# Encoder layer on one core: 30 convolution taps of one channel quarter as ScalarE copies with accumulating transfers, the output bank in halves, and other shares of the softmax scalings

## The chip, the cores and the metric

The kernel runs on one core of a Trainium2 chip. The metric is the device time of one execution in microseconds (us). Five engines work side by side: TensorE (PE: products and transposes into PSUM), VectorE (DVE), ScalarE (ACT), GpSimd (POOL) and SyncE (SP). Here POOL and SP mostly issue transfers (DMA). Each engine runs its own instructions in order and waits on semaphores for the others.

## The reference

One layer of a streaming encoder for 16 meta tokens, 1024 prompt frames and a stream of 32 sample frames, 1024 channels, float32. The change touches two of its parts, the depthwise convolution over a GLU and the attention over chunks of 64 frames:

```python
z = h @ w_in                                  # h = rmsnorm(x); all projections in one
glu = a_in[..., :D_CONV] * jax.nn.sigmoid(a_in[..., D_CONV:])          # 512 channels
y = depthwise_causal_conv(glu_ext, dw_w, dw_b)                         # 31 taps for each channel
conv = jax.nn.silu(layernorm(y, ln_g, ln_b))
s = q . k * HEAD_DIM ** -0.5 + bias            # 8 heads, 2 key heads; 16 meta + 3 x 64 keys
m = jnp.maximum(jnp.max(s, axis=-1, keepdims=True), sink)
p = jnp.exp(s - m)
denom = jnp.sum(p, axis=-1, keepdims=True) + jnp.exp(sink - m)
o = (p / denom) @ v
x = x + concat(conv, o) @ w_out               # then a gated feed-forward part and a last norm
```

The sink enters as one more key column. The attention of the meta tokens and that of the sample stream are jobs of their own, with a few keys each.

## The kernel before, in words

Everything lies channel by channel: a channel is a partition, the T = 1072 tokens run along the row, in three blocks of 336, 384 and 352. A float32 product is made of three passes over values split in a high and a low part (L239 hi x hi, L240 lo x hi, L241 hi x lo). A weight is split by `wsplit` (L221 to 230): ScalarE copies raw to whi (L224) and minus that to wlo (L228), and a transfer on POOL's queue adds raw onto wlo in memory (L229, an accumulating transfer).

The stages, by the time of the profile: input, statistics and first projections to 50 us; projections 50 to 168; attention 168 to 252, with the last projections between its steps; output projection and the convolution's norm 252 to 345; start of the feed-forward part 345 to 375; feed-forward 375 to 1030; its last norm and the stores to 1069.

Projections. `in_group` (L581) makes one output tile of 128 channels for one block of tokens, 24 products of some 3.9 us in all, in one of three PSUM banks called mm. VectorE takes the bank out later: L508 and L513 for the GLU, L533 for the queries (qp, with qm and qs for the meta and sample tokens). For the 512 convolution channels, in four quarters p, the GLU result lies in `glu[:, p]` and the sum over taps in `acc[:, p]`. `conv_taps` (L355 on) makes a quarter's taps ready: tap 0 is one operation acc = glu * w0 + b (L362), each further one acc = glu shifted * wk + acc (L365), on VectorE. `taps` (L370) gives them out after each group, at a low priority, so that VectorE's order, which a scheduler makes, fills them in between other work. SEGS says how a quarter is cut along the tokens: quarters 0 to 2 are one piece of 1090 columns (1072 and gaps between the streams), quarter 3 three pieces of 324, 384 and 382. The attention keeps its probabilities in the memory of `glu[:, 0]` and `glu[:, 1]`, so the taps of quarters 0 and 1 must be given out before it (L661).

Attention. The jobs (Meta, 11 chunks, Sample, 5 chunks) go through a pipeline of three steps (loop L937 to 969). In round i, job a of the round before gets its reciprocal (L701) and scalings: of its four tiles of probabilities, SCA[i] are scaled on ScalarE (L706) and the rest on VectorE (L704). The new job gets its scores S (PE, L732; Meta L786), the row maxima m on VectorE (L689, into sm) and the exponentials on ScalarE (L696). Job z of the round before that gets its output products (PE, L767 and L771; Meta L802) into a PSUM bank o. Then a is transposed (PE, L751 and L753 into pt; Meta L793), ScalarE copies the transposes (L758; Meta L796), and copies z's output from o into CA (`keep`, L775). FILL[i] pieces of the projection of the last two weights follow as work for PE, then taps for VectorE. There is one bank o, so a chunk's first output product waits for the copy of the chunk before. CA (128 x 4 x 1072) holds the attention output and is not used before the first `keep`. L546 is a sigmoid of 1040 columns between them, which changes ScalarE's function table there and back.

The orders of PE and ScalarE are written out by hand, as the program runs; those of VectorE, POOL and SP come from a scheduler with priorities. Statistics of a norm (`rms_steps`, L243 on) go over stat (L253 to 257), ScalarE's diag (L260) and a product R (L263).

Of the kernel before, what the change touches and what calls it, by code (L numbers as in the profile page):

```python
# [10 lines left out]
F32 = mybir.dt.float32  # L11
F32R = mybir.dt.float32r
AF = mybir.ActivationFunctionType
ALU = mybir.AluOpType
# [3 lines left out]
P = 128  # L18
# [6 lines left out]
T = NPR + NS  # L25
# [4 lines left out]
CW = 31  # L30
# [36 lines left out]
WLD = True  # L67
MANUAL = {mybir.EngineType.PE, mybir.EngineType.Activation}
MANEND = MANUAL | {mybir.EngineType.DVE}
SCA = [1, 3, 3, 3, 1, 1, 3, 2, 3, 3, 3, 1, 2, 3, 0, 1, 1, 3, 2, 2]  # L70
LN0 = 14
LNS = 21
FILL = [4, 6, 6, 2, 3, 3, 6, 1, 3, 3, 1, 4, 5, 0, 3, 6, 0, 3, 0, 3]
ORDER = [2, 3, 8, 9, 4, 5, 10, 11, 12, 13, 6, 7]
SEGS = (((0, 1, 2),), ((0, 1, 2),), ((0, 1, 2),), ((0,), (1,), (2,)))
CSD = ['12', '00']
AH = (1, 2, 1, 3, 5, 4, 5)
AG = (('00', '02'), ('h',), ('l',), ('10',), ('12',))
# [78 lines left out]
def body(nc, tc, cp, wp, xp, dp, io):  # L157
# [13 lines left out]
    def new(pl, name, *shape, dt=F32):  # L171
        return pl.tile([P, *shape], dt, tag=name, name=name)
# [7 lines left out]
    def pcol(name, i):  # L180
        o, _ = PRM[name]
        return prm[:, o + i:o + i + 1]
# [13 lines left out]
    acc = new(pc, "acc", NCV, ACCW)  # L196
    cG, pg = pool("glu", "left")
    glu = new(pg, "glu", NCV, EXTW)
# [81 lines left out]
    pa = cPS.__enter__()  # L280
# [51 lines left out]
    CA = new(pc_, "ca", 4, T)  # L332
# [24 lines left out]
    def conv_taps(p, a0, a1, b):  # L357
        e, a = glu[:, p, :], acc[:, p, a0:a1]

        def tap(k):  # L360
            if k == 0:
                nc.vector.tensor_scalar(out=a, in0=e[:, a0:a1], scalar1=pcol("cw", p * CW), scalar2=pcol("cb", p),  # L362
                                        op0=ALU.mult, op1=ALU.add)
            else:
                nc.vector.scalar_tensor_tensor(out=a, in0=e[:, a0 + k:a1 + k], scalar=pcol("cw", p * CW + k),  # L365
                                               in1=a, op0=ALU.mult, op1=ALU.add)

        tapq.append([b, a1 - a0, tap, 0, p])

    def taps(us, behind=None):  # L370
        spare[0] += us
        with tc.high_priority(offset=-1000000):
            while tapq and spare[0] > 0:
                spare[1] = (spare[1] + 1) % min(WAYS, len(tapq))
                ch = tapq[spare[1]]
                if behind:
                    with tc.issue_after(behind):
                        ch[2](ch[3])
                else:
                    ch[2](ch[3])  # L380
                ch[3] += 1
                if ch[3] == CW:
                    tapq.remove(ch)
                spare[0] -= (ch[1] + 120) / 960
        if not tapq:
            spare[0] = 0.0
# [96 lines left out]
    def in_mm(b, w, lead=0):  # L483
        n = TB[b][1] - lead
        hv, lv = (z.rearrange("p (a b) -> p a b", a=KD) for z in w)
        ps = mmt()[:, :n]
        for k in range(KD):
            mm3(ps, [k], lambda k: hv[:, k, :], lambda k: lv[:, k, :], lambda k: HI[b][:, k, lead:],
                lambda k: LO[b][:, k, lead:], k == 0, k == KD - 1)
            for g, at in zip(rms1, RM):  # L490
                if slot[0] in at:
                    next(g)
            slot[0] += 1
            yield ps

    def lead(c, b):
        return H0 if c >= 10 and b == 0 else 0
# [46 lines left out]
    def gate_all(p):  # L544
        for a, n in ((CW - 1, NPR), (CW - 1 + SOFF, NS)):
            nc.scalar.activation(glu[:, p, a:a + n], glu[:, p, a:a + n], AF.Sigmoid)  # L546
        for b in range(3):
            for lo_, hi_, o in pieces(b, CW - 1, SOFF):
                g = glu[:, p, o:o + hi_ - lo_]
                defer.append((g, rb[b][:, lo_:hi_]))  # L550

    def taps_of(p, b):
        for seg in SEGS[p]:
            if seg[-1] == b:
                conv_taps(p, OB[seg[0]][0], OB[b][0] + AW[b], seg[0])
        if b == 2:
            nc.sync.dma_start(d.cap[p], glu[:, p, NPR:NPR + CW - 1])
            nc.sync.dma_start(d.cas[p], glu[:, p, EXTW - CW + 1:EXTW])
# [5 lines left out]
    def undefer():  # L564
        while defer:
            g, rs = defer.pop(0)
            nc.vector.tensor_tensor(out=g, in0=g, in1=rs, op=ALU.mult)

    def flush():
        undefer()  # L570
        while pend and pend[0][1] in ready:
            c, b, ps = pend.pop(0)
            if c % 2:
                undefer()
            in_evac(c, b, ps)
            if c < 8 and c % 2:
                taps_of(c // 2, b)
            if c in (4, 6) and c in ORDER[NPRE:] and b == 2:
                gate_all(c // 2)

    def in_group(c, b, w, us=0.0):  # L581
        for ps in in_mm(b, w, lead(c, b)):
            pass
        flush()
        taps(us, gate[-1].ins if gate else None)
        pend.append((c, b, ps))

    def win(c):
# [69 lines left out]
    for _ in vr:  # L658
        pass
    flush()  # L660
    while any(t[4] < 2 for t in tapq):  # L661
        taps(1.0, gate[-1].ins)
    nc.sync.dma_start(d.kmp, kT[:, 0:NMETA])
# [45 lines left out]
        return pa.tile([P, 2, 256], F32, tag="s2", name="S", bufs=2)  # L709

    def o_tile():
        return pa.tile([P, 512], F32, tag="o", name="o", bufs=1)

    pts = [pa.tile([P, 2, 256], F32, tag=f"pt{i}", name=f"pt{i}") for i in range(2)]
    for q in pts:
        nc.vector.memset(q, 0.0)

    class Chunk:
# [43 lines left out]
        def outs(self):  # L762
            self.o = o_tile()
            c, m, n = self.c, self.m, self.n
            for kv in range(2):
                ks = slice(kv * 64, kv * 64 + 64)
                nc.tensor.matmul(self.o[ks, :256], va[:m, c, ks], ptb[kv][:m, 0, :], start=True, stop=n == m)  # L767
            for kv in range(2):
                ks = slice(kv * 64, kv * 64 + 64)
                if n > m:  # L770
                    nc.tensor.matmul(self.o[ks, :256], vb[:n - m, c - 1, ks], ptb[kv][:n - m, 1, :], start=False,  # L771
                                     stop=True)
# [5 lines left out]
    class Meta(Chunk):  # L778
# [19 lines left out]
        def outs(self):  # L798
            self.o = o_tile()
            for kv in range(2):  # L800
                ks = slice(kv * 64, kv * 64 + 64)
                nc.tensor.matmul(self.o[ks, :64], va[:16, 0, ks], ptb[0][:16, 0, kv * 64:kv * 64 + 64], start=True,  # L802
                                 stop=True)
# [4 lines left out]
    class Sample(Meta):  # L808
# [19 lines left out]
        def outs(self):  # L828
            self.o = o_tile()
            for kv in range(2):  # L830
                ks = slice(kv * 64, kv * 64 + 64)
                nc.tensor.matmul(self.o[ks, :128], vsa[:, ks], ptb[1][:, 0, kv * 128:kv * 128 + 128], start=True,
                                 stop=False)
            for kv in range(2):
                ks = slice(kv * 64, kv * 64 + 64)
                nc.tensor.matmul(self.o[ks, :128], vsb[:48, ks], ptb[1][:48, 1, kv * 128:kv * 128 + 128],
                                 start=False, stop=True)
# [73 lines left out]
    def ah_add(m2, i, b, ps):  # L911
        m, (t0, n) = 2 * m2 + i, OB[b]
        nc.scalar.copy(X[b][:, m, :], ps)
        if i == 1:
            nc.gpsimd.dma_start(X[b][:, m - 1:m + 1, :], d.xT[:, m - 1:m + 1, t0:t0 + n], accum_op=ALU.add)
# [17 lines left out]
    a, z = None, None  # L933
# [3 lines left out]
    for i in range(len(jobs) + 2):  # L937
        job = jobs[i] if i < len(jobs) else None
        if a:
            a.soft_b(SCA[i])  # L940
        if job:
            job.scores()
            job.soft_a()
            job.exps(0)
            job.exps(1)
        if z:
            z.outs()
        if a:
            a.trans()
            a.probs()  # L950
        if z:
            z.keep()
            kept[0] = i - 2
        for _ in range(min(FILL[i], left)):
            next(stream)
            left -= 1
        flush()
        taps(TA[i], (job or a or z).q[1][3])
        if not left and not pend and not defer:
            for _ in stream:  # L960
                pass
            next(later, None)
            ticks = len(jobs) + 2 - i
            for _ in range(AH[-ticks] if ticks <= len(AH) else 0):
                next(ahs, None)
            for q in adds:
                ah_add(*q)
            adds.clear()
        z, a = a, job
    for _ in later:  # L970
        pass
# [157 lines left out]
    with tc.tile_pool(name="psB", bufs=1, space=PSUM, reuse_waits="tile") as pf:  # L1129
# [332 lines left out]
        def scr(n):  # L1462
            nscr[0] += 1
            return scrs[nscr[0] % len(scrs)][:, :n]
# [62 lines left out]
        for i, (m, b) in enumerate([(m, b) for m in range(KD - 1, -1, -1) for b in (1, 2)] +  # L1527
# [6 lines left out]
            t0, n = YB[b]  # L1534
# [72 lines left out]
        for pos, (t0, n) in enumerate(ENDS):  # L1607
            last = pos + 1 == len(ENDS)
            for m in range(KD):
# [6 lines left out]
                to = parts[0] if m == 0 else scr(n)  # L1616
# [108 lines left out]
```

## Time and profile before

| | |
|---|---|
| three runs | 1068.04, 1068.41, 1074.01 us; median 1068.41 |
| the profiled execution | 1070.42 us, its span from first to last instruction 1068.6 |
| mean granted TensorE clock | 0.995 |
| bytes moved by DMA | 116.81 MB, 109 GB/s in the mean |
| chain of work that ended last | PE 58%, DVE 5%, DMA 2%, ACT 2% |

A row of the window view is one stretch of the time: its length, the busy time of each engine with its instructions in brackets, TensorE's granted clock as a share of full speed, the busy share of the 16 DMA engines, and GB/s. A row of the groups view names line, engine, operation, output and inputs with their shape, then the number, the busy time with the mean of one in ns, and the idle time ahead of it. A row of the waits view reads: engine, what it was about to do, what it waited for, total us, times, longest. A row of the timeline gives start and length, and in brackets the idle time ahead and who ended it. A row of the transfers view: target and source, queue, number, KB each, and the us from issue to landing.

### The profile page before, as it was taken

What the parts mean: (1) busy time and instruction counts of PE and PEld (TensorE: products, weight loads), DVE (VectorE), ACT (ScalarE), POOL (GpSimd) and SP (SyncE); (2) the same over time, 40 slices, a digit from 0 to 9 for tenths busy, and PEclk for the clock granted to TensorE, in tenths of its full rate; (3) what the DMA queues carried; (4) which work ended last, traced back from release to release, by engine and by line L of the source; (5) the groups of instructions that cost most, each with busy time, mean ns of one, the idle gap of its engine ahead of it and who ended that gap; (6) DMA issues with size and microseconds to landing.
All of it is one profiled execution on the core that took longest, in us unless ns stands there. A gap on an engine that the chain in (4) does not pass through costs nothing.

```text
span 1068.6 us, 19869 instructions
## 1 busy us (share of the span) xinstructions
PE 1041.1 (97%) x7737; PEld 1011.6 (95%) x7737; DVE 872.6 (82%) x1622; ACT 488.2 (46%) x1043; POOL 159.3 (15%) x189
## 2 busy tenths in 40 slices
PE   8999999989999999999999999999999999999996
PEld 7999997768999999999999999999999999999996
DVE  7799999999978988888888887888778865986635
ACT  8532225997676644433333343343337622532332
POOL 1112000001425112001000100100101041000042
PEclk9999999999999999999999999999999999999998
DMA  8343332114863122243233234233226894732104
GB/s 269 82 105 90 90 88 61 40 34 76 161 169 107 48 91 90 70 138 94 70 120 112 65 101 131 67 101 110 92 81 204 259 188 99 245 120 80 60 18 146
DMA packets 67030, 116.81 MB, mean 109 GB/s; under 512 B 10224, under 2 KB 43240, under 8 KB 66936
## 3 DMA queue, kind: packets, MB, share of 16 engines
q1 hardware_dynamic: 57112, 97.44, 29.2%
q0 software_dynamic: 9536, 17.89, 10.0%
q8 instruction: 61, 1.00, 0.4%
q14 instruction: 33, 0.27, 0.1%
q10 hardware_dynamic: 288, 0.22, 0.1%
HBM read 78.90 MB, written 27.51 MB: 100 GB/s over the span
## 4 chain that ended last, share of the span: by engine, by line
PE 58%; DVE 5%; DMA 2%; ACT 2%; issue 1%; POOL 0%; POOLq 0%; DVEq 0%; SPq 0%; ACTq 0%
PE mm L1208 49%; PE mm L239 3%; PE mm L240 3%; PE mm L241 3%; DMA rbg<-yq 1%; DVE traw L1225 1%; DVE x L1345 1%; DMA raw<-wdn 0%; DVE x L1595 0%; DVE bl L1145 0%; DMA x<-yq 0%; DVE tl L1145 0%; PE R L263 0%; DVE sl L1145 0%; ACT bh L1144 0%
## 5 line engine op out<-in xcount | busy, mean ns | idle before, releaser
L1208 PE MATMUL mm<-bh,sl 128*128 128x264 f32 (+1 forms) x912 | 215.0, 285 | 0.4 <-DVE x L1345 0.4
L365 DVE SCALAR_TENSOR_TENSOR acc<-glu,prm,acc 128x1090 f32<-128x1090 f32 (+3 forms) x180 | 168.0, 968 | 0.4
L1208 PEld LDWEIGHTS mm<-bh,sl 128*128 128x128 f32 x912 | 157.6, 189 | 0.7 <-DVE x L1345 0.7
L1208 PE MATMUL mm<-th,rawr 128*128 128x266 f32 (+1 forms) x640 | 121.3, 285 | 0.0
L1208 PE MATMUL mm<-bl,sl 128*128 128x264 f32 (+1 forms) x424 | 120.9, 285 | 0.0
L1208 PE MATMUL mm<-bh,wlo 128*128 128x264 f32 (+1 forms) x440 | 118.0, 285 | 0.0
L1345 DVE TENSOR_TENSOR x<-x,mm 128x264 f32<-128x264 f32 (+7 forms) x238 | 76.4, 347 | 50.3 <-PE mm L1208 50.2
L1208 PE MATMUL mm<-bh,whi 128*128 128x264 f32 (+1 forms) x440 | 113.1, 285 | 1.3 <-DVE x L1345 1.3
L239 PE MATMUL mm<-hi,whi 128*128 128x352 f32 (+3 forms) x312 | 104.6, 335 | 0.2 <-ACT hi L274 0.2
L240 PE MATMUL mm<-lo,whi 128*128 128x352 f32 (+3 forms) x312 | 102.1, 327 | 1.7 <-DVE lo L275 1.7
L241 PE MATMUL mm<-hi,wlo 128*128 128x352 f32 (+3 forms) x312 | 101.6, 326 | 0.0
L1208 PEld LDWEIGHTS mm<-th,rawr 128*128 128x128 f32 x640 | 101.2, 189 | 0.0
L1208 PE MATMUL mm<-th,sl 128*128 128x264 f32 (+1 forms) x352 | 93.1, 285 | 0.5 <-DVE x L1345 0.5
L1208 PE MATMUL mm<-tl,rawr 128*128 128x266 f32 (+1 forms) x320 | 91.4, 286 | 0.0
L1208 PEld LDWEIGHTS mm<-bh,wlo 128*128 128x128 f32 x440 | 80.7, 189 | 0.0
L1208 PEld LDWEIGHTS mm<-bh,whi 128*128 128x128 f32 x440 | 79.0, 189 | 1.7 <-DVE x L1345 1.3
L1208 PEld LDWEIGHTS mm<-bl,sl 128*128 128x128 f32 x424 | 79.9, 189 | 0.0
L1208 PE MATMUL mm<-bl,whi 128*128 128x264 f32 (+1 forms) x272 | 77.4, 285 | 0.0
L1208 PEld LDWEIGHTS mm<-th,sl 128*128 128x128 f32 x352 | 64.2, 189 | 0.6 <-issue 0.6
L1144 ACT CAST sl<-x 128x512 fp32r<-128x512 f32 (+1 forms) x41 | 29.7, 726 | 76.1 <-DMA x<-wup 40.3
L240 PEld LDWEIGHTS mm<-lo,whi 128*128 128x128 f32 x312 | 59.1, 189 | 3.4 <-DVE lo L275 3.1
L239 PEld LDWEIGHTS mm<-hi,whi 128*128 128x128 f32 x312 | 59.0, 189 | 1.7 <-ACT hi L274 0.7
(346 smaller groups left out, 2898.9 us busy)
## 6 DMA issues: line engine op xcount, KB each, us to landing
x<-wup SPq DMA_DIRECT2D x20, 512.0 KB, 4.4
x<-wup SPq DMA_DIRECT2D x40, 256.0 KB, 2.8
yq<-x SPq DMA_DIRECT2D x32, 264.0 KB, 2.8
wlo<-raw POOLq DMA_DIRECT2D x16, 512.0 KB, 4.5
raw<-win SPq DMA_DIRECT2D x12, 512.0 KB, 3.6
raw<-wdn SPq DMA_DIRECT2D x12, 512.0 KB, 3.8
rb<-yq SPq DMA_DIRECT2D x10, 528.0 KB, 4.4
yq<-gx SPq DMA_DIRECT2D x16, 264.0 KB, 4.7
```

Of the source, the lines that this page charges most:

```text
L239: nc.tensor.matmul(ps, whi(k), xhi(k), start=first and i == 0, stop=False)
L240: nc.tensor.matmul(ps, whi(k), xlo(k), start=False, stop=False)
L241: nc.tensor.matmul(ps, wlo(k), xhi(k), start=False, stop=last and i == n - 1)
L365: nc.vector.scalar_tensor_tensor(out=a, in0=e[:, a0 + k:a1 + k], scalar=pcol("cw", p * CW + k), in1=a, op0=ALU.mult, op1=ALU.add)
L1144: nc.scalar.copy(hi, raw)
L1208: nc.tensor.matmul(ps, w[:, j, :], x[:, j, :], start=first and j + i == 0, stop=j == 3 and i == 2, skip_group_check=True)
L1225: nc.vector.scalar_tensor_tensor(out=out[:, lo_:hi_], in0=x, scalar=pcol("g2", k), in1=z[:, lo_:hi_], op0=ALU.mult, op1=ALU.subtract)
L1345: nc.vector.tensor_tensor(out=z, in0=z, in1=banks[k][:, lo_:hi_], op=ALU.add)
```

## The change

Three things are changed. SCA, the share of ScalarE in the scalings, has 2 in place of 3 at nine rounds; seven scalings move to VectorE by it (widths 81, 145 and five times 209; in the other two rounds there is nothing to move). The bank o becomes one tile of two halves of 256 columns, which the jobs use in turn. And quarter 0 is cut into a piece of 324 columns, whose 31 taps stay on VectorE, and one of 766, the tokens from 336 on. Of that one tap 0 is as before, while taps 1 to 30 become a chain: ScalarE writes glu shifted * wk into one of three rows of CA, and an accumulating transfer on POOL's queue adds that row onto acc (odd k) or onto a second sum in the fourth row of CA (even k; tap 2 is written there by ScalarE itself). `chain_taps` gives out one tap after each projection group and what is left ahead of the attention, and `chain_end`, called in round i = 3, adds the second sum to acc on VectorE.

```diff
--- before.py
+++ after.py
@@ -67,12 +67,15 @@
 WLD = True
 MANUAL = {mybir.EngineType.PE, mybir.EngineType.Activation}
 MANEND = MANUAL | {mybir.EngineType.DVE}
-SCA = [1, 3, 3, 3, 1, 1, 3, 2, 3, 3, 3, 1, 2, 3, 0, 1, 1, 3, 2, 2]
+SCA = [1, 2, 2, 2, 1, 1, 2, 2, 2, 2, 2, 1, 2, 2, 0, 1, 1, 2, 2, 2]
 LN0 = 14
 LNS = 21
 FILL = [4, 6, 6, 2, 3, 3, 6, 1, 3, 3, 1, 4, 5, 0, 3, 6, 0, 3, 0, 3]
 ORDER = [2, 3, 8, 9, 4, 5, 10, 11, 12, 13, 6, 7]
-SEGS = (((0, 1, 2),), ((0, 1, 2),), ((0, 1, 2),), ((0,), (1,), (2,)))
+CHAINS = ((0, 1),)
+CHN = 1
+CHE = 3
+SEGS = (((0,), (1, 2)), ((0, 1, 2),), ((0, 1, 2),), ((0,), (1,), (2,)))
 CSD = ['12', '00']
 AH = (1, 2, 1, 3, 5, 4, 5)
 AG = (('00', '02'), ('h',), ('l',), ('10',), ('12',))
@@ -365,7 +368,40 @@
                 nc.vector.scalar_tensor_tensor(out=a, in0=e[:, a0 + k:a1 + k], scalar=pcol("cw", p * CW + k),
                                                in1=a, op0=ALU.mult, op1=ALU.add)
 
+        if (p, b) in CHAINS:
+            tap(0)
+            chq.append([p, a0, a1, 1])
+            return
         tapq.append([b, a1 - a0, tap, 0, p])
+
+    chq, chn = [], [0]
+
+    def chain_taps(n):
+        for _ in range(n):
+            if not chq:
+                return
+            p, a0, a1, k = chq[0]
+            z = CA[:, chn[0] % 3, T - (a1 - a0):]
+            half = CA[:, 3, T - (a1 - a0):]
+            to = (half, acc[:, p, a0:a1])[k % 2]
+            if k == 2:
+                z = half
+            else:
+                chn[0] += 1
+            nc.scalar.activation(z, glu[:, p, a0 + k:a1 + k], AF.Copy, scale=pcol("cw", p * CW + k))
+            if k != 2:
+                nc.gpsimd.dma_start(to, z, accum_op=ALU.add)
+            chq[0][3] += 1
+            if k == CW - 1:
+                chq.pop(0)
+                chain.append((acc[:, p, a0:a1], half))
+
+    chain = []
+
+    def chain_end():
+        for a, half in chain:
+            nc.vector.tensor_tensor(out=a, in0=a, in1=half, op=ALU.add)
+        chain.clear()
 
     def taps(us, behind=None):
         spare[0] += us
@@ -583,6 +619,7 @@
             pass
         flush()
         taps(us, gate[-1].ins if gate else None)
+        chain_taps(CHN)
         pend.append((c, b, ps))
 
     def win(c):
@@ -658,6 +695,7 @@
     for _ in vr:
         pass
     flush()
+    chain_taps(CW)
     while any(t[4] < 2 for t in tapq):
         taps(1.0, gate[-1].ins)
     nc.sync.dma_start(d.kmp, kT[:, 0:NMETA])
@@ -709,8 +747,10 @@
         return pa.tile([P, 2, 256], F32, tag="s2", name="S", bufs=2)
 
     def o_tile():
-        return pa.tile([P, 512], F32, tag="o", name="o", bufs=1)
-
+        onum[0] += 1
+        return obank[:, onum[0] % 2, :]
+
+    obank, onum = pa.tile([P, 2, 256], F32, tag="o", name="o", bufs=1), [0]
     pts = [pa.tile([P, 2, 256], F32, tag=f"pt{i}", name=f"pt{i}") for i in range(2)]
     for q in pts:
         nc.vector.memset(q, 0.0)
@@ -966,6 +1006,8 @@
             for q in adds:
                 ah_add(*q)
             adds.clear()
+        if i == CHE:
+            chain_end()
         z, a = a, job
     for _ in later:
         pass
```

Lines below the diff are shifted in the change: L365 is L368, L508 is L544, L533 is L569, L689 is L727, L701 is L739, L704 is L742, L229 is L232, L460 is L496.

VectorE at the end of the projections, around the evacuations of the last queries (qp) and the Meta softmax (L689, S with bme). Before:

```order
L365 SCALAR_TENSOR_TENSOR acc<-glu,prm,acc 128x1090 x3
L533 SCALAR_TENSOR_TENSOR qp<-mm,rb 128x6x64
L365 SCALAR_TENSOR_TENSOR acc<-glu,prm,acc 128x1090 x2
L533 SCALAR_TENSOR_TENSOR qp<-mm,rb 128x5x64
L533 SCALAR_TENSOR_TENSOR qs<-mm,rb 128x32
L365 SCALAR_TENSOR_TENSOR acc<-glu,prm,acc 128x1090 x2
L689 ISA glu,sm<-S,bme 128x17
L689 ISA sm 128x1
L365 SCALAR_TENSOR_TENSOR acc<-glu,prm,acc 128x1090
L508 TENSOR_TENSOR glu<-mm,rb 128x336
L701 RECIPROCAL sm<-sm 128x1
```

With the change:

```order
L569 SCALAR_TENSOR_TENSOR qp<-mm,rb 128x6x64
L368 SCALAR_TENSOR_TENSOR acc<-glu,prm,acc 128x1090 x2
L403 TENSOR_TENSOR acc<-acc,ca 128x766
L368 SCALAR_TENSOR_TENSOR acc<-glu,prm,acc 128x1090
L569 SCALAR_TENSOR_TENSOR qp<-mm,rb 128x5x64
L569 SCALAR_TENSOR_TENSOR qs<-mm,rb 128x32
L368 SCALAR_TENSOR_TENSOR acc<-glu,prm,acc 128x1090
L727 ISA glu,sm<-S,bme 128x17
L727 ISA sm 128x1
L544 TENSOR_TENSOR glu<-mm,rb 128x336
L368 SCALAR_TENSOR_TENSOR acc<-glu,prm,acc 128x1090
L739 RECIPROCAL sm<-sm 128x1
```

The join of the two sums (L403) stands ahead of the last evacuation, though the program calls it in round 3, and one tap of 1090 is left behind the Meta softmax.

VectorE in the softmax of the second and third chunk (145 and 209 columns). Before:

```order
L689 ISA glu,sm<-S,bt_289 128x145
L689 ISA sm 128x1
L365 SCALAR_TENSOR_TENSOR acc<-glu,prm,acc 128x1090
L738 COPY bt_289<-mv 128x4x16
L701 RECIPROCAL sm<-sm 128x4
L365 SCALAR_TENSOR_TENSOR acc<-glu,prm,acc 128x1090
L704 TENSOR_SCALAR pb_302<-pb_302,sm 128x145
L689 ISA glu,sm<-S,bt_288 128x209
L689 ISA sm 128x1
L689 ISA pb_299,sm<-S,bt_288 128x209
L689 ISA sm 128x1
L365 SCALAR_TENSOR_TENSOR acc<-glu,prm,acc 128x1090
```

With the change:

```order
L727 ISA sm 128x1
L778 COPY bt_289<-mv 128x4x16
L739 RECIPROCAL sm<-sm 128x4
L742 TENSOR_SCALAR pb_302<-pb_302,sm 128x145
L742 TENSOR_SCALAR pb_303<-pb_303,sm 128x145
L727 ISA glu,sm<-S,bt_288 128x209
L727 ISA sm 128x1
L727 ISA pb_299,sm<-S,bt_288 128x209
L727 ISA sm 128x1
L727 ISA pb_300,sm<-S,bt_288 128x209
```

The taps between the rows of the softmax are gone, and one scaling more stands there.

POOL at the end of the projections. Before:

```order
L459 MEMSET glu 128x30
L229 DMA wlo<-raw 128x1024 x2
L460 DMA glu<-cva 128x30
L229 DMA wlo<-raw 128x1024 x3
L870 DMA cal_2257<-ca 128x2x324
```

With the change:

```order
L393 DMA acc<-ca 128x766
L393 DMA ca<-ca 128x766
L393 DMA acc<-ca 128x766
L496 DMA glu<-cva 128x30
L232 DMA wlo<-raw 128x1024
L393 DMA ca<-ca 128x766
L393 DMA acc<-ca 128x766
L393 DMA ca<-ca 128x766
L232 DMA wlo<-raw 128x1024 x2
L910 DMA cal_2309<-ca 128x2x324
```

Between the transfers that finish weights (wlo) stand the last ones of the chain; those of even taps have ca as target, those of odd taps acc.

## The prediction

> **What bounds the kernel now.** I read the busy table of the page first, then the windows by stage, then the waits of TensorE and ScalarE between 165 and 260 us, then single rows.
>
> ```profile
> PE 1041.1 (97%) x7737; PEld 1011.6 (95%) x7737; DVE 872.6 (82%) x1622; ACT 488.2 (46%) x1043; POOL 159.3 (15%) x189
> 50.00:168.00 118.00, 118.00 (x732) 115.68 (x730) 111.42 (x136) 31.59 (x59) 15.76 (x24) 1.00 0.39 91
> 168.00:204.00 36.00, 32.72 (x223) 26.56 (x223) 34.55 (x99) 28.57 (x87) 0.84 (x1) 0.95 0.25 59
> 204.00:213.00 9.00, 8.66 (x68) 6.17 (x64) 8.89 (x33) 8.46 (x28) 0.00 (x0) 1.00 0.01 2
> 213.00:252.00 39.00, 34.08 (x257) 24.72 (x257) 39.00 (x146) 38.52 (x125) 3.28 (x4) 1.00 0.25 48
> ```
>
> A window row gives length, busy time of PE, PEld, DVE, ACT and POOL, then the granted clock and the DMA share. TensorE (PE) is the bound: in the projection stage (50 to 168) it is never idle, so what VectorE (DVE) saves there buys nothing by itself. The stage that the change can shorten is attention. From 168 to 204 PE idles 36.00 - 32.72 = 3.3 us and its clock is 0.95, some 36 x 0.05 = 1.8 us more; DVE is busy 34.55. From 204 to 252 it idles 0.3 + 4.9, with ScalarE (ACT) and DVE both full. All that attention could give back is about 10 us of 1068.6, 1%.
>
> ```profile
> PE o L767 <- ACT ca L775: 4.9, 8, 1.0
> PE pt L751 <- DVE glu L704: 1.4, 1, 1.4
> PE pt L751 <- ACT pb L706: 1.0, 2, 0.5
> ACT glu L696 <- DVE sm L689: 3.7, 5, 1.8
> ACT pb L696 <- DVE sm L689: 3.3, 2, 2.5
> 184.00:186.00 2.00, 1.23 (x8) 0.39 (x8) 2.00 (x9) 1.97 (x4) 0.00 (x0) 1.00 0.00 0
> 186.00:188.00 2.00, 0.72 (x4) 0.72 (x5) 2.00 (x9) 1.98 (x4) 0.00 (x0) 0.81 0.00 0
> 188.00:190.00 2.00, 2.00 (x10) 2.00 (x10) 2.00 (x5) 1.99 (x6) 0.00 (x0) 0.50 0.00 0
> 190.00:192.00 2.00, 2.00 (x15) 1.69 (x13) 1.63 (x3) 2.00 (x8) 0.00 (x0) 0.84 0.00 0
> ```
>
> PE's waits are for ACT's copy of a finished output (ca) and for softmax results; ACT in turn waits 7.0 us for DVE's row maxima (sm). The worst place is 184 to 188: PE idles 0.77 + 1.28 = 2.05 us, and behind it the clock falls to 0.81, 0.50 and 0.84, which costs 2 x (0.19 + 0.50 + 0.16) = 1.7 us, nearly all that the clock costs in this half.
>
> **The change part by part.** *Taps.* DVE loses 30 taps of 1090 and gains 30 of 324 and two halves of a first tap; ACT gains 30 copies of 766, POOL 29 accumulating transfers, DVE one add of 766.
>
> ```profile
> L365 DVE SCALAR_TENSOR_TENSOR acc<-glu,prm,acc 128x1090 f32<-128x1090 f32 x90 | 118.1, 1345 | 0.1
> L365 DVE SCALAR_TENSOR_TENSOR acc<-glu,prm,acc 128x324 f32<-128x324 f32 x30 | 16.6, 552 | 0.1
> 157.16 3.88 DVE L365 SCALAR_TENSOR_TENSOR acc<-glu,prm,acc 128x1090 f32<-128x1090 f32 x3
> 168.29 1.35 DVE L365 SCALAR_TENSOR_TENSOR acc<-glu,prm,acc 128x1090 f32<-128x1090 f32 x1
> 201.06 1.32 DVE L365 SCALAR_TENSOR_TENSOR acc<-glu,prm,acc 128x1090 f32<-128x1090 f32 x1
> L224 ACT CAST whi<-raw 128x1024 fp32r<-128x1024 f32 x16 | 16.8, 1049 | 37.6 <-issue 22.4 <-PE mm L240 15.2
> ```
>
> Back to back a 1090 tap takes 3.88/3 = 1.29 us. In the order of before, 74 of the 90 stand ahead of the Meta softmax and 16 behind it (168.29 to 201.06); in the change 59 and 30 short ones stand ahead, one behind. Ahead: 74 x 1.29 = 95.5 against 59 x 1.29 + 30 x 0.55 + 0.9 for the add (766/1090 of a tap) + 0.2 = 93.7: equal within 2 us, so DVE reaches the attention as before. Behind: 15 x 1.29 = 19.4 us leave the first half of attention. The ACT copies cost 766/1024 of a 1.05 cast, 0.78 each (bounds: 0.49 of a 209-wide scaling below, 1.05), 23 us in all, and ACT idles 118 - 31.6 = 86 us there: nothing. If that cover went, whi and wlo of the next weight would be late, but they have 9 us before PE asks.
>
> *The end of the chain.* Here the transfers count.
>
> ```profile
> wlo<-raw POOLq DMA_DIRECT2D x16, 512.0 KB, 4.5
> x<-xd POOLq DMA_DIRECT2D x4, 352.0 KB, 9.9
> 95.00:96.00 1.00, 1.00 (x7) 1.00 (x6) 1.00 (x3) 0.47 (x1) 0.00 (x0) 1.00 1.05 205
> 155.71 0.85 POOL L229 DMA_DIRECT2D wlo<-raw  x1 [1.74 <-ACT wlo L228]
> 161.42 2.61 DVE L365 SCALAR_TENSOR_TENSOR acc<-glu,prm,acc 128x1090 f32<-128x1090 f32 x2
> 168.19 0.18 DVE L689 CUSTOM_DVE_ANT_0 glu<-S,bme 128x17 f32<-128x17 f32 x1 [0.35 <-PE S L786]
> 170.38 0.31 ACT L706 ACTIVATE glu<-glu,sm 128x17 f32<-128x17 f32 x1 [0.23 <-DVE sm L701]
> 170.91 0.28 PE L793 MATMUL pt<-ident,glu 128*16 128x128 f32 x1
> ```
>
> The nearest row to a chain transfer (128 x 766 x 4 bytes = 383 KB, accumulating, on POOL's queue) is wlo<-raw: 512 KB, 4.5 us from issue to landing. At 205 GB/s, with all DMA engines busy (1.05), 383 KB take 1.9 us, call it 2; 29 of them some 57 us of 118 on top of a share of 0.39: they fit, one per 3.9 us group, on two targets in turn. But the last ones don't end in time. In the change POOL issues one wlo (155.71), then the transfers of taps 28, 29 and 30. wlo lands at 160.2, 28 at 162.2, 29 at 164.2; 30 writes where 28 wrote, so it is issued at 162.2 and lands about 166.4. The add that joins the two sums stands in DVE's order behind the last but one q evacuation and its two taps, where DVE arrives at 161.42 + 2.61 = 164.0, and waits for both sums. It is late by 2.4, and behind it stand a tap, the last q evacuation, a tap, and the Meta softmax (168.19): that one is 2.4 late too. ACT scales its result at 170.38 to 170.69 and PE transposes it at 170.91, so 0.2 us of slack are left: PE idles 2.2 us. A gap of 2.05 us cost 1.7 us of clock above; I take half of that, 0.9, since the gap comes whole instead of in two. Sum **+3.1**. Bounds: 0 (28 to 30 land without wlo ahead of them) and, at the 9.9 us of x<-xd (28 lands at 166.3, 30 at 176.2), 12.2 late, +12 and 1.7 of clock. I stay near the low end: size, queue and kind of wlo<-raw are those of the chain.
>
> The Trainium skill, TensorE: Matmul & The Clock Gate, section Part 1: The HAM clock gate, has the clock halved only after an idle window of about 3.4 us; the drop after 2.05 us of idle time in 4 us above does not fit that well. By the page the gap would cost no clock, and this term would be +2.2.
>
> *First half of attention.* With 19.4 us less on DVE in 36, minus three moved scalings (below), its row maxima no longer wait behind taps; the 7.0 us of ACT's waits shrink, the sigmoid block at 184.6 starts earlier than PE needs it, the 1.4 us wait for glu and the clock drop go. Of 3.3 + 1.8 = 5.1 us I give 4.0 back: the 1.1 left is PE's wait for ca, which hangs on ACT's own queue. **-4.0**, bounds 0 (ACT full there instead: 28.57 of 36) and -5.1.
>
> *Scalings.* Seven scalings leave ACT for DVE, widths 81, 145 and five of 209.
>
> ```profile
> L706 ACT ACTIVATE pb<-pb,sm 128x209 f32<-128x209 f32 x21 | 9.0, 485 | 0.0
> L704 DVE TENSOR_SCALAR pb<-pb,sm 128x209 f32<-128x209 f32 x20 | 5.8, 324 | 0.0
> L775 ACT COPY ca<-o 128x256 f32<-128x256 f32 x16 | 6.1, 381 | 0.6 <-PE o L771 0.6
> ```
>
> Three lie in the first half, covered by the taps that left. Four lie behind 204: ACT saves 4 x 0.43 = 1.7 (9.0/21 back to back), DVE pays 4 x 0.32 = 1.3 but has three 324 taps fewer there (-1.7). ACT is full there (38.52 of 39), but DVE is too (39.00 of 39), so only what both save counts: 0.4 by DVE, 1.7 by ACT; **-0.8**, bounds 0 and -1.7.
>
> *Bank halves.* PE's 4.9 us for ca are the price of one output bank: the next chunk's first product waits for a 0.38 us copy. With halves it writes other columns, but in the built order of the change that product still waits for ACT, on the copy of the chunk before; only its wait on PE itself is gone. So **0**; if the wait went, 8 x 0.38 = -3. The Trainium skill, PSUM — Partial Sum Buffer, section PSUM bank collisions raise a hardware error, tells to guard by bank and quadrant, not by address; by it two halves of one bank buy nothing, which is the value taken.
>
> *Order behind attention.* At the start of the feed-forward part the small rows of the last norm (stat) stand one or two rows earlier among DVE's transforms.
>
> ```profile
> PE R L263 <- ACT diag L260: 1.8, 1, 1.8
> 367.49 0.89 DVE L1225 SCALAR_TENSOR_TENSOR traw<-x,prm,traw 128x264 f32<-128x264 f32 x2
> 368.29 0.15 DVE L257 SCALAR_TENSOR_TENSOR stat<-stat 128x3 f32<-128x3 f32 x1
> ```
>
> PE waits 1.8 us once for what follows row L257; one 0.89 row less ahead of it could give that, but the transforms that it passes are needed next: **-0.5**, bounds 0 and -0.9.
>
> Sum: +3.1 - 4.0 - 0.8 + 0 - 0.5 = **-2.2** against the span of 1068.6, so 1066.4. The profiled execution took 1070.42 as the runs are timed, 1.8 over its span and 2.0 over the median 1068.41 of the three; span and median differ by 0.2, so the median forecast is **1066.2**.
>
> **The rivals.**
> *The chain lands late.* Ends on the slower side. Transfers that add read their target too, and 29 of them share engines with the weight loads; if one takes 7 us, half way from 4.5 to 9.9, tap 28 lands at 163.5, 30 at 170.5, the add is 6.5 late, PE idles 6.3 and pays the full 1.7 of clock: 1068.4 + 8.0 - 5.3 = 1071.1. It decides from a landing at 164.0 + 0.2 + (5.3 - 1.7) = 167.8 on, only 1.4 us behind my estimate. For it: x<-xd at 9.9. Against: wlo<-raw, the same kind, at 4.5 sixteen times.
> *The chain costs nothing and attention closes up.* Tap 30 lands by 164.5, PE's waits up to 204 go (-5.1), ACT's lead carries on behind 204 (-1.7), the wait at R goes half (-0.9): 1068.4 - 7.7 = 1060.7. For it: ACT's 7.0 us of waits all name DVE. Against: ACT's row of 38.52 of 39, and the order of POOL.
> *Nothing to be seen.* The chain's 3.1 is paid and the first half returns only the same 3.1, since ACT, full from 184 to 192 in the rows above, sets the pace: 1068.4 - 0.5 = 1067.9, or, if ACT's copies also push weights late, 1069. That the taps are not really taken off is excluded by the order.
>
> **How the numbers follow.** Forecast (1063 to 1068) 0.47, chain late (1068.5 to 1082) 0.27, attention closes up (1057 to 1063) 0.12, nothing to be seen (1067 to 1069.5) 0.14. The range, 1061 to 1073, leaves out the far half of the second rival at the low end and the late third of the first at the high end, 0.15 in all. 1%, 10.7 us, is about what a measurement of this kernel can tell from no change: below 1057.7 lies 0.02 (all idle time of attention gone), above 1079.1 lies 0.07 (transfers near 9.9), between them 0.91.
>
> **What would show it.** Right: the span up to 168 unchanged with PE busy 118 of 118 from 50 on; the add at L403 waiting for a POOL transfer 1.5 to 3 us and ending near 167; a new PE wait at the transpose of the Meta block of about 2 us; the waits pt<-glu L704 and the clock of 0.5 near 188 gone; PE's wait for ca still there, some 3 to 5 us; ACT still nearly full from 204 to 252, and DVE with some idle time ahead of 204. Wrong: an add that waits nothing or over 4 us; PE idle before 168; the wait for ca gone; or a length of the feed-forward part (375 to 1030) that differs by over 2 us, which no step here covers.

## The result, and the profile after

The change is slower: 1081.32 us median of 4 runs (1081.15 to 1085.46) against 1070.38 of 4 of the kernel before (1068.04 to 1074.01), a ratio of 1.0107 with a 95% interval of 1.0086 to 1.0128, some 11 us. The forecast was 1066.2, with 1061 to 1073 as range. The profiled execution is the longest of the four, 1085.46 with a span of 1083.7; the other three lie at 1081.2 to 1081.4, so its trace shows some 4 us more lost than they have. For sizes the timings of the experiments below are the better measure.

The windows of the change by stage, as for before:

```profile
50.00:168.00 118.00, 108.50 (x659) 105.28 (x658) 97.42 (x132) 51.84 (x84) 35.74 (x49) 0.96 0.85 170
168.00:204.00 36.00, 31.11 (x193) 27.39 (x191) 20.33 (x65) 15.90 (x47) 3.14 (x4) 0.91 0.44 92
204.00:213.00 9.00, 6.63 (x46) 5.14 (x48) 3.60 (x18) 8.97 (x25) 0.84 (x1) 1.00 0.10 19
213.00:252.00 39.00, 36.34 (x263) 26.31 (x262) 36.79 (x139) 35.07 (x114) 2.06 (x2) 0.96 0.15 33
375.00:1030.00 655.00, 651.30 (x5232) 649.54 (x5233) 526.94 (x872) 262.54 (x486) 68.53 (x80) 1.00 0.39 114
```

The surprise stands in the first row: PE, never idle from 50 to 168 before, now idles 9.5 us there at a clock of 0.96, and the DMA share went from 0.39 to 0.85. Of the waits of PE up to 300 us, these stand in the projections and the attention; those of VectorE show a second place:

```profile
PE nb L468 <- DMA acc<-ld: 9.5, 1, 9.5
PE o L807 <- ACT ca L815: 4.9, 8, 1.7
PE S L772 <- DVE sm L727: 3.0, 1, 3.0
PE pt L791 <- ACT pb L744: 2.2, 3, 0.9
PE pt L833 <- ACT glu L744: 1.2, 1, 1.2
```

```profile
DVE acc L403 <- DMA ca<-ca: 5.5, 1, 5.5
```

acc<-ld are the loads of the attention's bias tables: short rows gathered out of memory into the still unused part of acc, which the product nb (L468, L432 in before) turns into the bias tiles. No step of the prediction speaks of them. In before they were issued from 60.35 on, and nb ran at 68.88 without a wait, with its wait for them passed at 67.2. Windows of 2 us of the change around their place, and the transfers from 56 to 82 us:

```profile
58.00:60.00 2.00, 2.00 (x13) 2.00 (x12) 1.88 (x4) 0.95 (x2) 0.85 (x1) 1.00 1.10 206
62.00:64.00 2.00, 2.00 (x15) 2.00 (x14) 1.86 (x5) 0.00 (x0) 0.00 (x0) 1.00 1.12 183
68.00:70.00 2.00, 0.62 (x4) 0.34 (x3) 2.00 (x5) 0.00 (x0) 1.47 (x5) 1.00 1.13 214
72.00:74.00 2.00, 0.00 (x0) 0.00 (x0) 1.75 (x2) 0.00 (x0) 0.00 (x0) 0.50 1.04 202
76.00:78.00 2.00, 0.00 (x0) 0.00 (x0) 0.00 (x0) 0.00 (x0) 0.00 (x0) 0.50 0.31 71
```

```profile
acc<-ld SPq DMA_DIRECT2D x2, 208.0 KB, 12.3
ca<-ca POOLq DMA_DIRECT2D x2, 383.0 KB, 8.3
acc<-ca POOLq DMA_DIRECT2D x2, 383.0 KB, 8.7
```

The same view of before has, for the same loads:

```profile
acc<-ld SPq DMA_DIRECT2D x2, 208.0 KB, 3.9
```

With four chain transfers under way the DMA engines are full (shares of 1.04 to 1.13) until 74, and the loads take 12.3 us instead of 3.9. They also start 3.4 us later, at 63.76 instead of 60.35: SP's queue holds them until a small store whose data they read back (ld<-acc, 12 KB) has landed:

```profile
SPq L446 <- DMA ld<-acc: 2.0, 1, 2.0
```

PE stops from 68.6 to 78.1; its clock falls to half, so nb takes 3.33 us instead of 1.66.

The second place is the one that the prediction named. First POOL's last chain transfers, then VectorE's join and the row maximum of the Meta softmax:

```profile
166.86 0.85 POOL L232 DMA_DIRECT2D wlo<-raw  x1 [1.74 <-ACT wlo L231]
167.68 0.90 POOL L393 DMA_DIRECT2D ca<-ca  x1
168.50 0.95 POOL L393 DMA_DIRECT2D acc<-ca  x1
173.95 0.84 POOL L393 DMA_DIRECT2D ca<-ca  x1 [4.50 <-issue]
```

```profile
180.74 0.96 DVE L403 TENSOR_TENSOR acc<-acc,ca 128x766 f32<-128x766 f32 x1 [5.49 <-DMA ca<-ca]
184.64 0.17 DVE L727 CUSTOM_DVE_ANT_0 glu<-S,bme 128x17 f32<-128x17 f32 x1
```

Tap 28 goes out at 167.68, tap 30, which adds onto the same row, 6.3 us later, and its landing 6.7 us after that lets the join go at 180.74, 5.5 us after VectorE was there; the Meta softmax follows at 184.64.

To see where the time is lost and won, the times of four events in each trace in us (the start of nb; of the Meta scores; of the last group of output products of 256 columns; the span's end) and the differences between the last three ("attention" from the Meta scores to the last output, "behind it" from there to the end):

| kernel | nb | Meta scores | last output | span | attention | behind it |
|---|---|---|---|---|---|---|
| before | 68.9 | 167.9 | 255.2 | 1068.6 | 87.4 | 813.4 |
| change | 78.1 | 179.0 | 272.0 | 1083.7 | 93.0 | 811.7 |
| e2_late | 74.9 | 175.6 | 261.5 | 1072.9 | 86.0 | 811.4 |
| e9_early_join | 68.7 | 167.6 | 260.2 | 1070.7 | 92.6 | 810.5 |
| e7_early | 68.6 | 167.6 | 254.5 | 1069.7 | 86.9 | 815.2 |
| e3_nodma | 68.8 | 167.8 | 253.5 | 1063.8 | 85.8 | 810.3 |
| e6_short | 69.1 | 168.1 | 254.0 | 1064.8 | 85.9 | 810.8 |
| e11_sca0 | 68.7 | 167.6 | 254.8 | 1065.4 | 87.2 | 810.6 |
| e12_nosig | 68.3 | 167.1 | 250.2 | 1061.9 | 83.1 | 811.7 |
| e13_oldsca | 68.9 | 167.9 | 253.9 | 1066.0 | 86.0 | 812.1 |
| e4_sca | 68.3 | 167.3 | 256.5 | 1068.2 | 89.2 | 811.7 |
| e5_halves | 68.5 | 167.5 | 254.9 | 1067.2 | 87.4 | 812.4 |
| e16_wload | 71.2 | 172.0 | 257.9 | 1069.3 | 86.0 | 811.4 |
| e10_plain | 71.1 | 171.6 | 261.4 | 1075.2 | 89.8 | 813.8 |

The change loses 9.2 us at nb, 1.9 more by the Meta scores (1.7 of it in nb at the halved clock), 5.6 in the attention, and wins 1.7 behind it: 15.1 of span.

### The profile page after: what moved, and what is told of

Same layout as the page of the kernel before. It is cut to its first block, busy times and chain, and to the rows that moved or that the text cites. A ratio compares the mean times of both kernels' runs of the same rounds, so it can differ in the third digit from the quotient of the medians.

```text
span 1083.7 us, 19969 instructions
## 1 busy us (share of the span) xinstructions
PE 1045.1 (96%) x7737; PEld 1014.3 (94%) x7737; DVE 857.5 (79%) x1631; ACT 511.2 (47%) x1066; POOL 183.4 (17%) x218
## 4 chain that ended last, share of the span: by engine, by line
PE 58%; DVE 5%; DMA 1%; issue 1%; ACT 1%; POOL 0%; POOLq 0%; DVEq 0%; ACTq 0%; SPq 0%
PE mm L1250 51%; PE mm L242 2%; PE mm L244 2%; PE mm L243 2%; DVE traw L1267 1%; DMA rbg<-yq 1%; DMA gx<-yq 0%; DVE tl L1282 0%; DVE x L1637 0%; DMA x<-yq 0%; DVE bl L1187 0%; DVE x L1387 0%; ACT bh L1186 0%; PE R L266 0%; POOL rb L274 0%
## 5 line engine op out<-in xcount | busy, mean ns | idle before, releaser
L368 DVE SCALAR_TENSOR_TENSOR acc<-glu,prm,acc 128x324 f32<-128x324 f32 (+3 forms) x180 | 147.1, 834 | 1.9
```

## The experiments

All were timed beside the kernel before on the same chip; the ratios are against that, with a 95% interval. The expectations in us go by a before of 1068.4; it ran at 1070.5 to 1071.2 in the median there, so it is ratios that compare.

**e2_late: the join later.**

```diff
-CHE = 3
+CHE = 5
-            chain_end()
+            with tc.issue_after((job or a or z).q[1][3]):
+                chain_end()
```

> The change, with only the join of the two sums (the add of 766) placed later: behind the row maxima of round 5 instead of ahead of the last query evacuation. Theory A (two late waits make the loss: the bias tables, whose loads the chain's transfers slow down, about 9 to 11 us, and the join, about 7 us; the relief of VectorE gives some 3 back): the join's 7 us go, the bias wait stays: 1081 - 7 = 1074, with PE still idle some 9 us ahead of the product nb, and no wait of VectorE for a chain transfer ahead of the Meta softmax. Rival B (the join's place is harmless, since PE is late by then anyway and catches up on its own): 1080 to 1082.

1.0058 (1.0038 to 1.0077): 0.0049 under the change, 5.2 us. The attention is 7.0 us shorter in the trace, and the wait for the tables stays, 5.6 us here:

```profile
PE nb L468 <- DMA acc<-ld: 5.6, 1, 5.6
```

The join's place costs some 5 to 7 us, as theory A has it; rival B is refuted.

**e7_early and e9_early_join: the tables loaded earlier**, with the later join and with the join of the change.

```diff
-BS = ((1, 0), (1, 1), (2, 0), (2, 1))
+BS = ((0, 0), (0, 1), (2, 0), (2, 1))
```

> As the run with the later join, and the bias tables are loaded earlier: the two first steps of their preparation (line product, its store and the loads from it) stand behind the first and second projection group instead of the fourth and fifth, so that the loads have some 20 us instead of 10 before the product nb needs them. The chain of 30 taps is unchanged. Theory A: both waits are gone: 1074 - 10 = 1064 to 1066, PE busy without a gap from 50 to the Meta scores. Rival C (transfers that saturate the engines slow whatever is loaded in that stretch, so that the weights come late in place of the tables): one of the weights waits instead, PE idle 4 us or more between 50 and 168, 1070 or more.

> The change with only the earlier loads of the bias tables; the join stays ahead of the last query evacuation, as in the change. It completes the square of the two repairs. Theory A (two separate waits that add up): 11 us less than the change, about 1071, and VectorE waits for the chain 5 to 7 us ahead of the Meta softmax; against the run with both repairs, 5 us more. Rival E (the join waits only because all of it came late): the join finds both sums there, no wait over 1 us, 1066 to 1067.

e7_early: 0.9976 (0.9963 to 0.999); e9_early_join: 1.0028 (1.0017 to 1.0039). The four kernels make a square. The earlier tables are worth 0.0079 with the old join and 0.0082 with the later one, 8.5 to 8.8 us; the later join is worth 0.0049 and 0.0052. They add up: two separate waits. In e7_early PE is full ahead of the attention although the DMA share is even higher than in the change (row of 50 to 168), so it is not the load on the engines that costs but what is due while it lasts; rival C is refuted. In e9_early_join the join waits as long as in the change, though PE is 11 us earlier; rival E is refuted. First the stage row of e7_early, then the join of e9_early_join:

```profile
50.00:168.00 118.00, 118.00 (x735) 116.51 (x735) 107.96 (x143) 54.69 (x87) 38.79 (x53) 1.00 0.94 190
```

```profile
169.33 0.96 DVE L403 TENSOR_TENSOR acc<-acc,ca 128x766 f32<-128x766 f32 x1 [5.48 <-DMA ca<-ca]
```

**e3_nodma: without the transfers.**

```diff
-            if k != 2:
-                nc.gpsimd.dma_start(to, z, accum_op=ALU.add)
```

> The change without the 29 accumulating transfers (their additions are left out; ScalarE's 30 copies, the first tap, the join and all else stay). Theory A: no wait for the bias tables, none at the join; what is left is VectorE's relief in the attention, 1063 to 1066. Rival D (it is not the transfers but ScalarE's copies, which push the weights' splits and the bias copies back): 1075 or more.

0.9964 (0.9952 to 0.9975). Both waits are gone with ScalarE's copies still there, so the copies cost nothing (rival D is refuted), and the whole loss is the transfers'. What is left is the gain from relieving VectorE and from its other order: 1.6 us of attention and 3.1 behind it.

**e10_plain: transfers that don't add.**

```diff
-                nc.gpsimd.dma_start(to, z, accum_op=ALU.add)
+                nc.gpsimd.dma_start(to, z)
```

> The change with its 29 transfers as plain copies (they overwrite their target in place of adding to it; bytes, number, queue and waits are the same). Theory A1 (an adding transfer costs the engines more than its bytes, since it reads its target too): the DMA share from 50 to 168 falls from 0.85 to 0.6 or 0.7, the wait for the tables to under 5 us, the time to 1070 to 1075. Rival A2 (bytes and packets alone load the engines): share 0.8 or more, 1079 to 1083.

1.003 (1.0016 to 1.0044). Its stage row and its transfers from 50 to 168, against those of the change in the same stretch:

```profile
50.00:168.00 118.00, 115.80 (x705) 112.56 (x704) 103.84 (x138) 52.87 (x85) 29.98 (x51) 0.99 0.66 189
```

```profile
acc<-ca POOLq DMA_DIRECT2D x14, 383.0 KB, 4.7
acc<-ld SPq DMA_DIRECT2D x2, 208.0 KB, 8.0
```

```profile
acc<-ca POOLq DMA_DIRECT2D x13, 383.0 KB, 5.8
```

Copies of the same size load the engines to 0.66 instead of 0.85: if the 0.39 of before is taken off both, the chain's part is 0.27 for 28 copies and 0.46 for 26 additions. The wait for the tables is 2.2 us, that of the join 3.0. Theory A1 holds.

**e16_wload: the weight load behind the table loads** (on top of e2_late; bl holds the last of the table loads).

```diff
-            if b == 0:
+            if b == 0 and i != 2:
                 fetch()
+            elif b == 0:
+                with tc.issue_after(bl[-1]):
+                    fetch()
```

> As the run with the later join only, and the weight load that stands ahead of the loads of the bias tables on SP's queue is issued behind them. Theory A (the tables are slow since all engines are full of the chain's transfers): PE still waits 3 us or more ahead of nb, 1073 to 1077. Rival L (they are slow since their queue is busy with the 512 KB ahead of them, which the chain makes slow): the wait falls under 1 us, 1066 to 1068, if the weight is not late then.

1.0005 (0.9995 to 1.0014), 5.7 us less than e2_late; PE waits 2.7 us for the tables, in place of 5.6. Neither was right alone: half of the wait in the traces, and more in the timings, is the 512 KB ahead on the same queue. With that moved, the table loads take 4.0 us, as in before (3.9), with the chain still running. What stays is their late start, at 63.93 instead of 60.35: SP's queue waits 5.4 us for the small store, where it waited 0.6 in before:

```profile
SPq L448 <- DMA ld<-acc: 5.4, 1, 5.4
```

**e6_short: a chain that fits.** It starts behind the seventh group and has 22 taps; the other 8 go to VectorE, and the sums lie in two rows of CA; two adds join them, as late as in e2_late.

```diff
+HOLD = 7
-CHE = 3
+CHE = 5
+CHK = 23
+            tapq.append([b, a1 - a0, tap, CHK, p])
-            z = CA[:, chn[0] % 3, T - (a1 - a0):]
-            half = CA[:, 3, T - (a1 - a0):]
-            to = (half, acc[:, p, a0:a1])[k % 2]
-            if k == 2:
-                z = half
+            z = CA[:, chn[0] % 2, T - (a1 - a0):]
+            to = CA[:, 2 + k % 2, T - (a1 - a0):]
+            if k < 3:
+                z = to
...
+        grp[0] += 1
+        if grp[0] > HOLD:
+            chain_taps(CHN)
```

> As the run with the later join, but the chain starts behind the seventh projection group, when the bias tables are there, and has 22 taps; the 8 others of that piece go back to VectorE (0.9 us each), and the chain adds onto two sums of its own, joined by two adds. Theory A: no wait for the tables; VectorE carries 7 us more into the attention than the change does, 12 less than before: 1065 to 1068. Rival C (any chain beside the weight loads costs): over 1070.

0.9969 (0.9954 to 0.9983), the same as without any transfer. The idea of the change is worth some 0.3% once nothing waits for the chain.

**e4_sca and e5_halves: the two small parts alone**, on the kernel before (the SCA line of the diff; the two hunks of `o_tile`).

> The kernel before with only the seven scalings moved from ScalarE to VectorE. Theory A (they help only where VectorE has room, and it has none in the kernel before): within 1.5 us of before, on either side. Rival F (ScalarE is what the attention waits for, whatever VectorE does): 2 us or more faster.

> The kernel before with only the output bank in two halves. Theory A (the first product of a chunk still waits for the copy of the chunk before): within 1 us of before, and the wait of PE for ca stays, 8 times and some 5 us. Rival G (the halves free it): the wait is gone and the kernel 2 to 3 us faster.

e4_sca: 1.0 (0.999 to 1.0009). In its trace attention is 1.8 us longer than before and what follows it 1.7 shorter, the wait of 1.8 us at R being gone there. e5_halves: 0.9981 (0.9969 to 0.9994), but its attention is 87.4 us as before, with the same wait:

```profile
PE o L769 <- ACT ca L777: 4.8, 8, 1.0
```

So the halves free nothing in the attention, as theory A has it. Where the 0.2% of the timing comes from, the trace does not show (0.4 us lie ahead of 168, 1.0 behind 255, where the program is the same); it stays open.

**e12_nosig: what holds the relief back** (on top of e6_short).

```diff
-            nc.scalar.activation(glu[:, p, a:a + n], glu[:, p, a:a + n], AF.Sigmoid)
+            nc.scalar.activation(glu[:, p, a:a + n], glu[:, p, a:a + n], AF.Copy)
```

> As the run with the chain of 22 taps behind the seventh group and the later join, with the sigmoid of 1040 columns between the chunks replaced by a plain copy of the same columns (the sigmoid of that quarter is left out), so that the two loads of ScalarE's function table around it, 1.28 us each, go away. Theory I (the relief of VectorE gave 1.5 us in place of 4 because ScalarE's stay at the sigmoid, with its two table loads, holds the next copies and scalings back, PE waiting 0.83 for pb and 1.71 for ca behind it): both waits go and the run is 2 to 3 us shorter, 1064. Rival J (PE's waits there come from the chunks' softmax whatever is between them): under 0.7 us.

0.9933 (0.9919 to 0.9948), 0.0036 or 3.9 us under e6_short (2.9 in the traces), with an attention of 83.1. PE's two waits behind the sigmoid in e6_short, and the same two products in e12_nosig:

```profile
186.37 0.33 PE L796 MATMUL pt<-ident,pb 128*128 128x128 f32 x1 [0.83 <-ACT pb L749]
190.81 0.65 PE L812 MATMUL o<-glu,va 128*64 128x256 f32 x4 [1.71 <-ACT ca L820]
```

```profile
184.47 0.27 PE L796 MATMUL pt<-ident,pb 128*128 128x128 f32 x1
187.08 0.65 PE L812 MATMUL o<-glu,va 128*64 128x256 f32 x4
```

Both waits are gone; theory I holds. The copy in the sigmoid's place takes as long as the sigmoid (1.20 us against 1.19), so it is the two table loads that go, and the attention is 2.8 us shorter. ScalarE around them in e6_short:

```profile
183.08 0.37 ACT L820 COPY ca<-o 128x256 f32<-128x256 f32 x1
183.47 1.28 ACT L585 ACT_TABLE_LOAD   x1
184.76 1.19 ACT L585 ACTIVATE glu<-glu 128x1040 f32<-128x1040 f32 x2
186.33 1.28 ACT L739 ACT_TABLE_LOAD   x1
```

The Trainium skill, ScalarE: Activation LUTs, section What ACT_TABLE_LOAD costs, gives some 1283 ns for the load, which agrees with the rows, and some 1380 ns of drain besides. The rows show no such drain: the first load starts 0.02 us behind the copy ahead of it, and the sigmoid 0.01 us behind the load.

**e11_sca0 and e13_oldsca: other shares of the scalings** (on top of e6_short: `SCA = [1, 0, 0, 0, 0, 0, 0, 0, 1, 1, 2, ...]`, and that of before).

> As the run with the chain of 22 taps behind the seventh group and the later join, with the scalings of rounds 1 to 7 all on VectorE (and one of four on ScalarE in rounds 8 and 9), where VectorE now has room. Theory A: PE's waits for pb from ScalarE's scalings (2.2 us) shrink, ScalarE reaches the sigmoid and what is behind it earlier: 1 to 2 us less than that run, 1065. Rival H (ScalarE's exponentials and copies alone set its pace, the scalings fit in its waits): no difference, within 0.7.

> As the run with the chain of 22 taps behind the seventh group and the later join, with the shares of scalings of the kernel before (3 in place of 2 on ScalarE). Theory K (more scalings on VectorE help once the taps are off it): 1 us or more longer, 1068. Rival H (they fit in either engine's idle time): no difference, within 0.7.

e11_sca0: 0.9969 (0.9956 to 0.9982); e13_oldsca: 0.9943 (0.9927 to 0.996), which the interval of e6_short, in another session, touches; the attention is 86.0 against 85.9 in the traces. In e11_sca0 the wait for pb shrinks from 2.2 to 0.8 us and that for ca grows from 5.2 to 6.4. Rival H holds: where a scaling is done hardly matters here. Both e13_oldsca and e6_short beat the kernel before by 0.3 to 0.6%.

## Why the prediction was wrong

**"29 of them some 57 us of 118 on top of a share of 0.39: they fit"** is the step that failed. The sum itself was good (0.48 + 0.39 = 0.87; 0.85 was measured, with 26 of the 29 in the stage), but the step put the cost for PE in this stage at nothing. A mean of 0.85 has emptier stretches and full ones in it, here a share of 0.98 to 1.34 from 58 to 74, and in that stretch stood the transfers that PE needs soon: a small store and the loads that read it back, for a product due at 68.9, with less than 2 us of slack in before. The text looked for what would be late among the weights, which "have 9 us before PE asks", and never listed the other transfers due in the stage. It cost 9.2 + 1.9 us in the trace, 8.5 to 8.8 in the timed square, and is shown by e3, e7, e9 and e16. "PE idle before 168" was one of the signs of being wrong that the prediction gave, an add that waits "over 4 us" another; both came.

**The end of the chain, +3.1**: the mechanism was right, place, order and all; the size was off by two. With PE's 11.1 us of delay taken off, VectorE came to the join when the prediction says (175.25 - 11.1 = 164.1; 164.0), and tap 30 went out 0.7 us late (162.9; 162.2). The term that was mis-sized is the time that tap 30 takes: put at 4.2 us, measured at 6.7. A weight load of 512 KB (raw<-woa, issued at 171.52) was under way beside it, the DMA share being 0.92 to 1.13 from 172 to 178; the prediction does not list it. No run takes that load away, so that it is the reason is not shown. The join came 5.5 late instead of 2.4. It cost 7.0 in one pair of traces (93.0 against 86.0) and 5.7 in the other (e9 against e7), 5.2 to 5.6 in the timings. PE did not stop at the Meta transpose first, but at the scores of the first chunk (3.0), whose second bank the Meta softmax had not read out yet, then at the transpose (1.2); most of the rest is the clock:

```profile
182.00:184.00 2.00, 0.00 (x0) 0.00 (x0) 2.00 (x4) 0.00 (x0) 0.00 (x0) 1.00 0.03 4
184.00:186.00 2.00, 1.14 (x6) 0.93 (x6) 2.00 (x5) 1.11 (x1) 0.00 (x0) 0.61 0.69 216
186.00:188.00 2.00, 0.83 (x5) 0.82 (x4) 1.49 (x11) 1.76 (x10) 0.00 (x0) 0.50 0.12 46
188.00:190.00 2.00, 2.00 (x8) 2.00 (x8) 0.61 (x3) 1.26 (x7) 0.00 (x0) 0.50 0.00 0
```

From 190 to 192 PE is busy throughout at 0.69. By its busy time alone it loses 0.39 x 1.14 + 0.50 x 0.83 + 0.50 x 2.00 + 0.31 x 2.00 = 2.5 us by the clock, where 0.9 was put; the +2.2 that the prediction gives for a gap without a price in clock is not borne out at this gap of 3.0 us. This part is nearly the rival "the chain lands late" (6.5 late, 8.0 lost). The time measured lies in that rival's band, to which 0.27 had been given, but only because the wait for the tables, which the rival does not hold, came on top.

**First half of attention, -4.0**: the relief of 19 us of VectorE gave 1.4 to 1.6 over the whole attention (e2, e3, e6 against before), scalings included. In e3 and e6 the clock drop did go (1.00 from 168 to 204; in e7, e11 and e13 it was 0.95, as before), but not PE's idle time (3.4 us there, 3.3 before): PE now waits for ScalarE, and e12 names the block, the two table loads at the sigmoid. The prediction had this case as its bound at 0, "ACT full there instead"; ScalarE's order set the pace without its being full (28.92 of 36 in e3).

**Scalings, -0.8**: nothing to be seen (e4: 1.0; e13 against e6: 0.1 us of attention in the trace). **Bank halves, 0**: right (4.8 and 4.9 us of wait). **Order behind attention, -0.5**: the wait of 1.8 at R falls to 0.3 in the change and away in e3, e4, e6, e7, e9 and e13; of the 1.3 to 3.1 us that these traces win behind the attention (e7's aside, which waits 3.5 us once in the feed-forward part) it can be up to 1.8; the rest is not settled.

Put together with the sizes in the traces: 11.1 + 7.0 - 1.4 - 1.7 = 15.0, of 15.1. The split of the attention into 7.0 and 1.4 rests on e2_late, so this sum agrees by the way it is made. A run of its own checks it: e3_nodma lies 0.0143, 15.3 us, under the change, and the two waits make 13.7 to 14.4 us in the timings of the square.

## What to carry to other kernels

Transfers that fit on the average can still fill the DMA engines for the 10 us in which a small load is due. Before a stage is given more transfers, list every load and store in it with the time at which it is needed. Then start the extra ones behind the last with little slack (e6), bring that one forward (e7), or take large loads off the queue ahead of it (e16). Price a transfer by one that runs beside the others of its stretch, and let nothing wait for its end in an engine's fixed order. When one engine is relieved, look at which wait stands next behind it before the gain is counted.

## What was not expected of the hardware

An adding transfer between two places of on-chip memory loaded the DMA engines some 1.8 times as much as a copy of the same bytes (26 of them 0.46 of the 16 engines over 118 us, 28 copies 0.27, 383 KB each, with the share of before taken off) and took 5.8 us instead of 4.7. Behind a 512 KB load on their own queue, short-row loads of 208 KB went from 3.9 to 12.3 us beside the adding transfers (6.5 in e2_late), and to 8.0 beside copies; with that load moved behind them it was 4.0 (e16). SP's queue itself was held up: one issue of a table load in the change took 5.58 us, where most take 0.5 to 0.7.

```profile
68.46 0.57 SPq L458 DMA_DIRECT2D acc<-ld  x1
69.07 5.58 SPq L457 DMA_DIRECT2D acc<-ld  x1
```
